# One level of Strassen's scheme in the first matmul of three feed-forwards

## The chip, the core and the metric

The kernel runs on one core of a Trainium2 chip. The metric is the device time of the program in microseconds (us), the median of a few runs. One execution was recorded by the hardware profiler; all rows below are from it. PE is TensorE's matmuls, PEld its weight loads, DVE is VectorE, ACT ScalarE, SP the engine whose queue issues the DMAs.

## The reference

Two transformer-like blocks on 512 tokens of 1024 features, float32: the first has two layers (pooling, latent attention and a linear recurrence, gated and summed), the second one layer (a state-space branch and a dilated attention). Each of these three layers ends in a feed-forward of 4096 hidden features, and the change is in these:

```
# first block, twice
h = rms_norm(x, g_ffn[l])
x = x + jnp.square(jax.nn.relu(h @ w_ff1[l])) @ w_ff2[l]
# second block, once
h = layer_norm(alpha * h + mix, ln1_g, ln1_b)
f = jnp.square(jax.nn.relu(h @ w_up)) @ w_down
h = layer_norm(alpha * h + f, ln2_g, ln2_b)
```

## The kernel before

Activations lie with features on the 128 partitions and the 512 tokens along the columns: 1024 features are eight tiles of 128 x 512. Each float32 number is held as a high and a low part that the matmul takes in one pass, so that a product of two tiles is three matmuls (`mm3`: high x high, high x low, low x high). `split` makes the parts: ScalarE copies the high part, VectorE subtracts it from the number for the low part. `X` holds the eight pairs of input tiles (`xh`, `xl`).

Weights come as panels of 128 x 1024 in the order of use. `load` takes a raw slot (class W, 4 slots), issues one DMA on SP's queue, and splits the panel into two tiles of class H (8 slots). A panel of the first matmul (`ff1`, `up`) holds the eight stationary blocks for 128 hidden features; `mmk` runs 8 x 3 = 24 matmuls over it, each of 128 rows, 128 stationary columns and 512 tokens, into one PSUM bank. Working tiles are of class T (57 slots of 128 x 528), PSUM has eight banks (class P).

`ffn` (L986) goes over four chunks of 1024 hidden features. In a chunk it makes eight hidden tiles (24 matmuls, ReLU on ScalarE, square on VectorE, split), then multiplies them by eight panels of the second matmul (`ff2`, `dn`) and adds the results to eight sums `acc`. The last chunk's second matmul goes over the token halves one after the other (`parts`), in 256 columns, and its results go to `last` and `done`, which close the layer. In the second block the first four panels of `up` are also run by token halves (`mmh`, `head=4`), so that TensorE has work on the first half while the layer norm of the second is made (`layer_norm`, `done1` in `out2`).

Ahead of the feed-forward, `mix1` runs the output projection: for each of eight tiles 24 matmuls, then VectorE adds the residual, ScalarE and VectorE split the sum with the gain `g_ffn` into `xh`, `xl`, and the sum stays in a T tile (`xn`) until the end of the feed-forward. The scale 1/rms of a token is put in at the end, since ReLU squared lets it pass.

The program is recorded first and then ordered by a list scheduler (`order`) that knows rough costs and the number of slots of each class; loads and splits of weights get a lead of 250 instructions. Each engine then runs its list in that order. The scheduler may move a plain copy from ScalarE to VectorE and back (`other`). All instructions are emitted in one place, so they carry the line L505; the groups of the profile are told apart by tiles.

Of the kernel before, what the change touches and what calls it, by code (L numbers as in the profile page):

```python
# [7 lines left out]
F32 = mybir.dt.float32  # L8
# [34 lines left out]
# ---------------------------------------------------------------- small vectors, one column per 128 features  # L43
# [65 lines left out]
def cells(v):  # L109
    """The parts of its tile that a view covers: halves of the partitions by blocks of 128 columns."""  # L110
# [19 lines left out]
# from an instruction's end to the start of one that waits for it on another engine, ns  # L130
# [19 lines left out]
class Prefix:  # L150
    """Point updates, and the least prefix sum over the first n positions."""
# [19 lines left out]
    def low(self, n):  # L171
        """min over k <= n of the sum of the first k positions."""
# [14 lines left out]
class Recorder:  # L187
# [8 lines left out]
    # -- tiles  # L196
    def open(self, sizes):
        """sizes: class -> (count, columns, space). A slot takes one tile after the other, of either type."""
        self.sizes, self.pools, self.protos = sizes, {}, {}
        for c, (n, cols, space) in sizes.items():  # L200
            p = self.tc.tile_pool(name=f"sl{c}", bufs=1, space=space, reuse_waits="tile")
            self.pools[c] = p, p.__enter__()
            for dt in (F32,) if c in "PSW" else (F32, F32R):
                self.protos[c, dt] = self.place(c, 0, dt)
# [40 lines left out]
    def record(self, eng, meth, args, kw):  # L245
# [43 lines left out]
        o.pri = i - (self.LEAD if i > 200 and isinstance(outs[0], View) and outs[0].tile.cls in ("W", "H") else 0)  # L289
# [1354 lines left out]
```

## Time and profile before

| what | value |
|---|---|
| median of three runs | 2553.19 us (2552.67 to 2555.08) |
| span of the profiled execution | 2552.5 us |
| TensorE busy | 2528.0 us, 12166 matmuls |
| VectorE busy | 1600.6 us |
| ScalarE busy | 1067.0 us |
| weights and scratch read from HBM | 241.39 MB |

Busy time is the union of an engine's instructions. A matmul's recorded duration includes its way through the array and overlaps the next one, so the pace of matmuls is read from the starts of two rows, not from their mean duration. The three feed-forwards stand at 365.61 to 724.32, 1078.18 to 1448.20 and 2167.58 to 2544.60 us of the span.

### The profile page before, as it was taken

To read this page: it belongs to the slowest core of one execution; us is meant where nothing else is said; L and a number is where in the kernel's file an instruction comes from. 1 tells how busy PE (TensorE), PEld (TensorE's weight loads), DVE (VectorE), ACT (ScalarE), POOL (GpSimd) and SP (SyncE) were. 2 spreads that over 40 slices of the span, in tenths; PEclk is the share of its full clock that TensorE was granted. 3 is DMA by queue.
4 is the path that set the end of the run, shared out by engine and by line. 5 is a ranking of instruction groups with operands and counts; after the bars stand their busy time and mean duration, and the time that the engine had idled before them with its cause. 6 is when DMAs were issued, how large, how long until landed. Compare 5 with 4: busy or idle time off the path is not lost.

```text
span 2552.5 us, 31172 instructions
## 1 busy us (share of the span) xinstructions
PE 2528.0 (99%) x12166; PEld 2063.3 (81%) x12166; DVE 1600.6 (63%) x2708; ACT 1067.0 (42%) x1796; POOL 0.2 (0%) x4
## 2 busy tenths in 40 slices
PE   8999999999999999999999999999999999999997
PEld 6888888888888888888888977777778789888887
DVE  7878554433578685544345747688999787633455
ACT  5545343322335453333233334356755743522332
POOL 0000000000000000000000000000000000000000
PEclk9999999999999999999999999999999999999998
DMA  4123332222331223323233221334422442222231
GB/s 156 64 81 96 119 100 91 96 94 95 116 110 56 81 91 122 93 91 99 92 102 121 77 75 50 100 110 151 133 91 99 149 165 83 69 97 92 102 104 34
DMA packets 83971, 251.93 MB, mean 99 GB/s; under 512 B 9520, under 2 KB 12720, under 8 KB 83824
## 3 DMA queue, kind: packets, MB, share of 16 engines
q1 hardware_dynamic: 83824, 249.95, 30.2%
q8 instruction: 95, 1.56, 0.2%
q14 instruction: 52, 0.43, 0.1%
HBM read 241.39 MB, written 8.52 MB: 98 GB/s over the span
## 4 chain that ended last, share of the span: by engine, by line
PE 97%; DVE 1%; ACT 1%; issue 0%; DMA 0%; SPq 0%; ACTq 0%; DVEq 0%
PE P L505 97%; DVE T L505 1%; ACT T L505 1%; DVE H L505 0%; DVE S L505 0%; DMA T<-in_x_dram 0%; ACT H L505 0%; ACT L505 0%; DVE xl L505 0%; SPq L505 0%; ACT xh L505 0%; ACTq L1640 0%; DVE xh L505 0%; DVEq L505 0%; ACTq L505 0%
## 5 line engine op out<-in xcount | busy, mean ns | idle before, releaser
L505 PE MATMUL P<-xh,H 128*128 128x512 f32 (+1 forms) x3912 | 1257.9, 396 | 8.8 <-DVE xh L505 6.1
L505 DVE TENSOR_TENSOR H<-W,H 128x1024 fp32r<-128x1024 f32 (+1 forms) x395 | 477.0, 1213 | 649.2 <-PE P L505 436.3
L505 PE MATMUL P<-T,H 128*128 128x512 f32 (+1 forms) x3924 | 880.2, 378 | 0.0
L505 PEld LDWEIGHTS P<-xh,H 128*128 128x128 f32 x3912 | 725.8, 189 | 181.0 <-issue 12.3
L505 ACT ACTIVATE H<-W 128x1024 fp32r<-128x1024 f32 (+1 forms) x389 | 407.5, 1052 | 1002.0 <-PE P L505 931.7
L505 PEld LDWEIGHTS P<-T,H 128*128 128x128 f32 x3924 | 695.2, 188 | 145.4 <-issue 1.5
L505 PE MATMUL P<-xl,H 128*128 128x512 f32 (+1 forms) x1968 | 772.2, 395 | 1.1 <-DVE xl L505 0.9
L505 PEld LDWEIGHTS P<-xl,H 128*128 128x128 f32 x1968 | 371.6, 189 | 87.0 <-issue 5.5
L505 DVE TENSOR_TENSOR T<-T,T 128x512 f32<-128x512 f32 (+5 forms) x600 | 363.4, 622 | 27.3 <-ACT T L505 13.1
L505 PE MATMUL P<-T,T 128*128 128x256 f32 (+7 forms) x1536 | 279.0, 311 | 0.0
L505 ACT ACTIVATE T<-T 128x512 fp32r<-128x512 f32 (+4 forms) x329 | 191.4, 591 | 164.5 <-DVE T L505 158.1
L505 PEld LDWEIGHTS P<-T,T 128*128 128x128 f32 (+2 forms) x1536 | 210.7, 184 | 37.2 <-issue 17.1
L505 ACT ACTIVATE T<-P 128x512 f32<-128x512 f32 (+6 forms) x281 | 148.9, 549 | 153.1 <-PE P L505 152.6
L505 DVE TENSOR_TENSOR T<-T,P 128x512 f32<-128x512 f32 (+2 forms) x190 | 109.3, 578 | 51.7 <-PE P L505 36.4
L505 DVE TENSOR_TENSOR T<-P,T 128x512 f32<-128x512 f32 (+5 forms) x224 | 131.4, 612 | 12.4 <-PE P L505 7.4
L505 ACT ACTIVATE T<-T,T 128x128 f32<-128x128 f32 (+1 forms) x320 | 121.2, 455 | 11.1 <-DMA T<-fscr 9.1
L505 DVE TENSOR_TENSOR T<-T 128x512 f32<-128x512 f32 (+3 forms) x109 | 75.3, 692 | 50.3 <-ACT T L505 50.2
L505 DVE SCALAR_TENSOR_TENSOR T<-T,P 128x512 f32<-128x512 f32 (+1 forms) x120 | 67.4, 575 | 29.0 <-PE P L505 23.2
L505 PE MATMUL P<-c,T 128*128 128x128 f32 (+1 forms) x436 | 74.0, 271 | 0.2 <-ACT T L505 0.2
L505 DVE SCALAR_TENSOR_TENSOR T<-P,half,T 128x510 f32<-128x510 f32 (+1 forms) x96 | 70.3, 743 | 0.6 <-ACT T L505 0.3
L505 PEld LDWEIGHTS P<-c,T 128*128 128x128 f32 (+1 forms) x436 | 54.5, 140 | 14.7 <-DVE T L505 0.9
L505 DVE SCALAR_TENSOR_TENSOR T<-T,T 128x512 f32<-128x512 f32 (+2 forms) x69 | 46.8, 685 | 12.7 <-ACT T L505 11.9
(74 smaller groups left out, 731.5 us busy)
## 6 DMA issues: line engine op xcount, KB each, us to landing
W<-in_w_dram SPq DMA_DIRECT2D x382, 512.0 KB, 3.4
T<-fscr SPq DMA_DIRECT2D x64, 256.0 KB, 4.8
T<-in_w_dram SPq DMA_DIRECT2D x24, 256.0 KB, 4.1
T<-in_x_dram SPq DMA_DIRECT2D x16, 256.0 KB, 4.7
W<-in_w_dram SPq DMA_DIRECT2D x10, 384.0 KB, 3.1
T<-in_c_dram SPq DMA_DIRECT2D x8, 256.0 KB, 4.5
xscr<-T SPq DMA_DIRECT2D x8, 256.0 KB, 2.2
T<-xscr SPq DMA_DIRECT2D x8, 256.0 KB, 3.9
```

The lines of the kernel that those rows point to most:

```text
L505: self.out(o, getattr(getattr(self.nc, o.eng), o.meth)(*[res(a) for a in o.args], **{k: res(v) for k, v in o.kw.items()}))
```

## The change

The first matmul of a feed-forward takes two panels together, 256 hidden features, and splits it as a 2 x 2 product of blocks: the features in pairs of tiles, the hidden features in two halves of 128, and the tokens in two halves of 256. Of the eight block products of this shape it makes seven, in Winograd's form, from sums of weight blocks and sums of token halves. Each product is a sum over four pairs of input tiles, three matmuls each: 12 matmuls of 256 columns. In one layer of the first block 16 pairs of panels are made so; in the second block 14, since its first four panels are still run as before.

- `wforms` loads two panels, makes four sums of 512 columns on VectorE, and splits seven forms of 512 columns.
- `xforms` makes the sums of token halves for two input tiles, and splits them; two of the forms overwrite the second half of an `X` tile. It runs in the output projection of the first block and in the layer norm of the second.
- `up` runs the seven products into three PSUM tiles. One of them (`a`) collects four products and is copied out by ScalarE after each of three and at the end; VectorE adds the other two.
- ReLU squared is now one VectorE instruction, max(u, 0) x u, or min for the tile that comes out negated.
- `ffn` records four pairs first, and then one pair after every second panel of the second matmul; the hidden tiles of the next chunk are made while those of this chunk are used.
- Classes W and H become one class W of 16 slots.
- The residual sum goes to a scratch in HBM (`rscr`) and is read back at the end of the feed-forward; in the second block the scaled residual is made in the layer norm.

```
-            self.open({"T": (57, T + 16, SB), "W": (4, 1024, SB), "H": (8, 1024, SB), "S": (48, 8, SB), "P": (8, T, PSUM)})
+            self.open({"T": (57, T + 16, SB), "W": (16, 1024, SB), "S": (48, 8, SB), "P": (8, T, PSUM)})
...
+    def wforms(self, name, p):
...
+        for i, t in enumerate((r1, r2)):
+            self.S.dma_start(t, bass.AP(tensor=self.wp.tensor, offset=off + (2 * p + i) * P * w, ap=[[w, P], [1, w]]))
...
+        a11, a22, a12, a21 = r1[:, L], r1[:, R], r2[:, L], r2[:, R]
+        f11, f12 = both(a11), both(a12)
+        s1 = add(a22, a21)
+        s2 = add(s1, a11)
+        g2, g1 = both(s2), both(s1)
+        s3 = add(a11, a21)
+        g3, f22 = both(s3), both(a22)
+        return f11, f12, both(add(s2, a12)), f22, g1, g2, g3
...
+    def xforms(self, j, v1, v2, raw=True):
...
+        t, u = self.F(), self.F()
+        V.tensor_tensor(t[:, L], v1[:, L], v1[:, R], op=ALU.subtract)
+        V.scalar_tensor_tensor(u[:, L], t[:, L], -1.0, v2[:, R], op0=ALU.mult, op1=ALU.subtract)
+        V.tensor_tensor(u[:, R], v2[:, R], v1[:, R], op=ALU.subtract)
+        V.scalar_tensor_tensor(t[:, R], u[:, L], -1.0, v2[:, L], op0=ALU.mult, op1=ALU.subtract)
+        if raw:
+            self.split(t[:, L], h1[:, R], l1[:, R])
+        g = self.splitR(u)
...
+    def product(self, ps, w, q, start, stop):
+
+        for j in range(4):
+            b = slice(j * P, (j + 1) * P)
+            self.mm3(ps, w[q][0][:, b], w[q][1][:, b], *self.G[j][q], start and j == 0, stop and j == 3, skip_group_check=True)
+
+    def up(self, name, p):
...
+        self.product(a, w, 0, True, False)
+        A.activation(f[:, L], a, AF.Copy)
+        self.product(b, w, 1, True, True)
+        V.tensor_tensor(f[:, L], f[:, L], b, op=ALU.add)
+        self.product(a, w, 5, False, False)
+        A.activation(f[:, R], a, AF.Copy)
+        self.product(c, w, 4, True, False)
+        self.product(a, w, 6, False, False)
+        A.activation(g[:, R], a, AF.Copy)
+        V.tensor_tensor(g[:, R], g[:, R], c, op=ALU.add)
+        self.product(a, w, 3, False, True)
+        A.activation(g[:, L], a, AF.Copy)
+        self.product(c, w, 2, False, True)
+        V.tensor_tensor(f[:, R], f[:, R], c, op=ALU.add)
+        return f, g
...
+        for i in range(4):
+            up(i)
+        for ch in range(3):
             for c in range(8):
-                if ch == 3:
-                    break
                 ps = self.PS()
-                self.mmk(ps, self.load(n2, ch * 8 + c), hid)
+                self.mmk(ps, self.load(n2, ch * 8 + c), hids[ch])
...
+                if c % 2 == 0:
+                    up(4 * ch + 4 + c // 2)
```

What the scheduler makes of it, at two places. TensorE near the start of the first feed-forward, before: the end of the first panel and the start of the second; `ones` and `c` stand for the sums over the partitions and the broadcast of the scale.

```order
L505 MATMUL P_767_3350<-xh_78,H_756_3274 128x512
L505 MATMUL P_767_3350<-xh_80,H_748_3204 128x512
L505 MATMUL P_767_3350<-xl_81,H_748_3204 128x512
L505 MATMUL P_767_3350<-xh_80,H_756_3274 128x512
L505 MATMUL P_775_3396<-c_62,S_773_3390 128x128 x4
L505 MATMUL P_777_3403<-xh_66,H_753_3241 128x512
L505 MATMUL P_777_3403<-xl_67,H_753_3241 128x512
L505 MATMUL P_777_3403<-xh_66,H_761_3311 128x512
```

After, in the same feed-forward where pairs and down-panels alternate: the end of one product into the PSUM tile P_946 and the start of the next into it.

```order
L505 MATMUL P_946_4293<-T_815_3528,W_926_4177 128x256
L505 MATMUL P_946_4293<-T_817_3540,W_926_4177 128x256
L505 MATMUL P_946_4293<-T_815_3528,W_926_4177 128x256
L505 MATMUL P_959_4382<-T_850_3737,W_939_4256 128x512
L505 MATMUL P_959_4382<-T_852_3749,W_939_4256 128x512
L505 MATMUL P_959_4382<-T_850_3737,W_945_4291 128x512
L505 MATMUL P_959_4382<-T_843_3702,W_939_4256 128x512
L505 MATMUL P_959_4382<-T_845_3714,W_939_4256 128x512
L505 MATMUL P_959_4382<-T_843_3702,W_945_4291 128x512
L505 MATMUL P_946_4293<-T_757_3211,W_928_4200 128x256
L505 MATMUL P_946_4293<-T_759_3219,W_928_4200 128x256
```

Before, each bank is filled once and left; after, six matmuls of a down-panel (P_959) stand between two products into the same tile.

VectorE at the end of the output projection of the first layer, before: P_762 is the eighth projection's result, xl_81 the low part that the first panel needs last.

```order
L505 TENSOR_TENSOR H_761_3311<-W_744_3175,H_753_3241 128x1024
L505 TENSOR_TENSOR T_671_2744<-P_757_3276,T_671_2744 128x512
L505 SCALAR_TENSOR_TENSOR xl_79<-T_671_2744,vec,xh_78 128x512
L505 TENSOR_TENSOR T_735_3111<-T_735_3111,T_765_3332 128x512
L505 TENSOR_TENSOR H_766_3348<-W_749_3212,H_758_3278 128x1024
L505 TENSOR_TENSOR T_681_2792<-P_762_3313,T_681_2792 128x512
L505 SCALAR_TENSOR_TENSOR xl_81<-T_681_2792,vec,xh_80 128x512
```

After, from the addition of the eighth projection's result (P_792) on:

```order
L505 TENSOR_TENSOR T_696_2875<-P_792_3406,T_696_2875 128x512
L505 TENSOR_TENSOR W_802_3457<-T_768_3268,W_802_3457 128x512
L505 TENSOR_TENSOR T_808_3487<-T_801_3453,W_775_3309 128x512
L505 SCALAR_TENSOR_TENSOR T_811_3498<-T_799_3436,T_807_3480 128x256
L505 TENSOR_TENSOR W_809_3491<-T_780_3341,W_809_3491 128x512
L505 TENSOR_TENSOR xl_81<-T_807_3480,xh_80 128x512
L505 TENSOR_TENSOR T_811_3498<-T_807_3480,T_796_3424 128x256
L505 TENSOR_TENSOR T_739_3120<-T_739_3120,T_812_3507 128x512
L505 SCALAR_TENSOR_TENSOR T_799_3436<-T_811_3498,T_807_3480 128x256
L505 TENSOR_TENSOR T_817_3540<-T_811_3498,T_815_3528 128x512
L505 TENSOR_TENSOR W_816_3536<-W_737_3109,W_816_3536 128x512
L505 TENSOR_TENSOR xl_79<-T_799_3436,xh_78 128x256
```

Before, the low part follows the addition at once; after, weight sums, low parts of weights (W) and combinations of token halves (T_811, T_799) stand between, and the second half of xl_79 is written anew at the end.

## Rows read from the trace of the kernel before

**Rows 1.** The page's parts 1 and 2: span, busy time by engine, clock in 40 slices.

```profile
span 2552.5 us, 31172 instructions
PE 2528.0 (99%) x12166; PEld 2063.3 (81%) x12166; DVE 1600.6 (63%) x2708; ACT 1067.0 (42%) x1796; POOL 0.2 (0%) x4
...
PEclk9999999999999999999999999999999999999998
```

**Rows 2.** The page's part 4, the chain that ended last.

```profile
PE 97%; DVE 1%; ACT 1%; issue 0%; DMA 0%; SPq 0%; ACTq 0%; DVEq 0%
```

**Rows 3.** TensorE's waits: for whom, us in total, times, the longest.

```profile
PE P L505 <- DVE xh L505: 6.1, 1, 6.1
```

**Rows 4.** Windows: length, busy PE, PEld, DVE, ACT, POOL, clock, DMA share, GB/s.

```profile
320.90:365.61 44.71, 44.71 (x195) 36.23 (x193) 24.90 (x32) 17.87 (x24) 0.00 (x0) 1.00 0.32 105
365.61:724.32 358.71, 358.71 (x1554) 290.17 (x1552) 162.10 (x193) 113.64 (x144) 0.00 (x0) 1.00 0.31 100
1078.18:1448.20 370.02, 370.02 (x1832) 309.76 (x1831) 175.04 (x268) 115.43 (x160) 0.00 (x0) 1.00 0.30 96
2167.58:2544.60 377.02, 368.64 (x1880) 311.36 (x1878) 183.56 (x311) 123.52 (x188) 0.00 (x0) 0.99 0.24 81
```

**Rows 5.** Windows of matmuls of 512 columns alone: a down stretch, an up stretch.

```profile
412.18:456.66 44.48, 44.48 (x194) 36.03 (x192) 15.37 (x17) 9.60 (x10) 0.00 (x0) 1.00 0.30 95
456.66:501.44 44.78, 44.78 (x193) 36.09 (x192) 20.13 (x24) 16.30 (x22) 0.00 (x0) 1.00 0.29 94
```

**Rows 6.** Matmuls of 256 columns: timeline of PE (start, length), then windows.

```profile
2487.08 11.59 PE L505 MATMUL P<-T,H 128*128 128x256 f32 x96
2498.51 11.45 PE L505 MATMUL P<-T,T 128*128 128x256 f32 x96
...
2487.08:2498.51 11.43, 11.43 (x97) 11.42 (x96) 5.73 (x9) 1.23 (x2) 0.00 (x0) 1.00 0.01 2
2498.51:2509.80 11.29, 11.29 (x99) 11.29 (x97) 3.39 (x8) 0.00 (x0) 0.00 (x0) 1.00 0.01 1
```

**Rows 7.** Groups by shape, whole span: count, busy us, mean ns, idle before.

```profile
L505 DVE TENSOR_TENSOR H<-W,H 128x1024 fp32r<-128x1024 f32 x382 | 465.9, 1224 | 644.3 <-PE P L505 431.5 <-issue 210.3 <-ACT H L505 1.3
L505 ACT ACTIVATE H<-W 128x1024 fp32r<-128x1024 f32 x376 | 397.5, 1060 | 978.9 <-PE P L505 916.8 <-issue 55.7 <-DMA W<-in_w_dram 3.9
L505 DVE TENSOR_TENSOR T<-T,T 128x512 f32<-128x512 f32 x290 | 193.0, 685 | 8.0 <-ACT T L505 5.6 <-PE P L505 0.3
L505 ACT ACTIVATE T<-T 128x512 fp32r<-128x512 f32 x178 | 111.0, 630 | 63.6 <-DVE T L505 60.6
L505 DVE TENSOR_TENSOR T<-T,P 128x256 f32<-128x256 f32 x80 | 33.0, 418 | 36.0 <-PE P L505 35.3
L505 ACT ACTIVATE T<-P 128x256 fp32r<-128x256 f32 x23 | 8.8, 387 | 4.7 <-PE P L505 4.7
```

**Rows 8.** Timeline of DVE: queued instructions of one shape, start and length.

```profile
181.99 1.89 DVE L505 TENSOR_TENSOR T<-T,T 128x512 fp32r<-128x512 f32 x3
...
2535.68 1.42 DVE L505 SCALAR_TENSOR_TENSOR T<-P,T 128x256 f32<-128x256 f32 x4 [0.79 <-PE P L505]
```

**Rows 9.** Timeline at the start of the first feed-forward, PE, DVE and ACT.

```profile
365.61 0.39 PE L505 MATMUL P<-xh,H 128*128 128x512 f32 x1
...
366.72 0.68 DVE L505 TENSOR_TENSOR T<-P,T 128x512 f32<-128x512 f32 x1
368.20 0.75 DVE L505 SCALAR_TENSOR_TENSOR xl<-T,vec,xh 128x512 fp32r<-128x512 f32 x1 [0.79 <-ACT xh L505]
...
367.44 0.72 ACT L505 ACTIVATE xh<-T,vec 128x512 fp32r<-128x512 f32 x1 [0.52 <-DVE T L505]
```

**Rows 10.** The layer norm before the third feed-forward: PE with its waits; a window.

```profile
2181.86 0.71 PE L505 MATMUL P<-c,S 128*128 128x128 f32 x4 [0.67 <-DVE S L505]
2184.10 0.88 PE L505 MATMUL P<-xh,H 128*128 128x256 f32 x4 [1.53 <-ACT xh L505]
...
2185.10:2188.60 3.50, 3.50 (x19) 3.50 (x20) 3.13 (x9) 3.40 (x8) 0.00 (x0) 0.59 0.02 5
```

More of the change, by code (lines that the diff above doesn't have):

```diff
@@ L202, in open @@
             self.pools[c] = p, p.__enter__()
-            for dt in (F32,) if c in "PSW" else (F32, F32R):
+            for dt in (F32,) if c in "PS" else (F32, F32R):
                 self.protos[c, dt] = self.place(c, 0, dt)
@@ L288, in record @@
         o.alt = self.other(o)
-        o.pri = i - (self.LEAD if i > 200 and isinstance(outs[0], View) and outs[0].tile.cls in ("W", "H") else 0)
+        o.pri = i - (self.LEAD if i > 200 and isinstance(outs[0], View) and outs[0].tile.cls == "W" else 0)
         self.ops.append(o)
@@ L548, in load, with both, add @@
         return lambda a, b: (hi[:, a:b], lo[:, a:b])
+    def wforms(self, name, p):
+        V, off, w = self.V, WOFF[name][0], 1024
+        r1, r2 = self.new("W", w), self.new("W", w)
+        for i, t in enumerate((r1, r2)):
+            self.S.dma_start(t, bass.AP(tensor=self.wp.tensor, offset=off + (2 * p + i) * P * w, ap=[[w, P], [1, w]]))
+        L, R = slice(0, T), slice(T, w)
+        def both(x):
+            hl = self.new("W", w, F32R)
+            self.split(x, hl[:, L], hl[:, R])
+            return hl[:, L], hl[:, R]
+        def add(a, b):
+            o = self.F()
+            V.tensor_tensor(o, a, b, op=ALU.add)
+            return o
+        a11, a22, a12, a21 = r1[:, L], r1[:, R], r2[:, L], r2[:, R]
[6 more added lines that the diff above has]
+        return f11, f12, both(add(s2, a12)), f22, g1, g2, g3
@@ L593, in stack, with mm3 @@
         return t
[L595 removed]
+    def mm3(self, out, lh, ll, rh, rl, start, stop, **kw):
         mm = self.E.matmul
[L597 to L599 removed]
+        mm(out, lh, rh, start=start, stop=False, **kw)
+        mm(out, lh, rl, start=False, stop=False, **kw)
+        mm(out, ll, rh, start=False, stop=stop, **kw)
     def mmk(self, out, w, xs, off=0, toks=None):
@@ L1429, in proj, with mid @@
             add(c, t, tk)
+        y2 = [self.F() for _ in range(8)]
+        self.G, t1 = [None] * 4, []
+        def mid():
+            for j, t in enumerate(t1):
+                self.split(t, *(x[:, HALVES[1]] for x in X[2 * j]))
         def done1(tk):
@@ L1436, in fin @@
                 V.tensor_tensor(X[k][1][:, tk], v, h.bitcast(F32), op=ALU.subtract)
+                A.activation(y2[k][:, tk], v, AF.Copy, scale=ALPHA)
+                if tk.start and k % 2:
+                    t1.append(self.xforms(k // 2, y[k - 1], y[k], False))
             return self.layer_norm([v[:, tk] for v in y], sums[tk.start], "ln1_g", fin, tk.start > 0)
         self.parts("out2", 0, HALVES, proj, done1)
-        y2 = self.residual()
         def last(c, acc, tk):
@@ L1457, in done @@
             return self.layer_norm([v[:, tk] for v in y2], sums[tk.start], "ln2_g", fin2, tk.start > 0)
-        self.ffn("up", "dn", HALVES, last, done, head=4, acc=y2)
+        self.ffn("up", "dn", HALVES, last, done, y2, 4, mid)
     def residual(self):
@@ L1508, in _tiles, with _quads @@
     return [np.concatenate([_fm(w, slice(c * P, (c + 1) * P), K, P) for c in range(a, a + per)], axis=1) for a in range(0, n, per)]
+def _quads(w):
+    out = []
+    for c in range(0, w.shape[1], 256):
+        a, b = (_fm(w, slice(c + i, c + i + P), 8, P).reshape(P, 4, 2, P) for i in (0, P))
+        for i in range(2):
+            out.append(np.concatenate([x.reshape(P, T) for x in (a[:, :, i], b[:, :, 1 - i])], axis=1))
+    return out
 def _bd(w, j):
```

79 lines of the change are left out of this document (53 added, 26 removed).

## The prediction

> **What bounds the kernel now.** The page comes first. TensorE is busy 99% of the span, VectorE 63%, ScalarE 42%, and TensorE's clock is granted in full nearly throughout [rows 1]. The chain that ended last lies on TensorE for 97% [rows 2]. Its longest wait for another engine is 6.1 us, at the program's start [rows 3]. Then the stretches: in the three feed-forwards TensorE is busy for all of 358.71 and 370.02 us and for 368.64 of 377.02, while VectorE works for under half of each [rows 4]. So a matmul column taken from TensorE there shortens the program, as long as the other engines keep handing over in time; and VectorE has some 190 us to spare in each.
>
> The profiled execution spans 2552.5 us [rows 1]; the median of the runs is 2553.19, 0.7 us outside the span. The sum below is taken off 2553.2.
>
> **TensorE's work.** Two hidden blocks (256 hidden features) take two panels of 24 matmuls of 512 columns before, and seven products of 4 x 3 = 12 matmuls of 256 columns after: 48 large against 84 small. What matters is the pace, start to start, in stretches with one shape only. 512 columns: the eight up-panels (24 matmuls each) from 456.66 to 501.44 take 44.78 us for 192, 233.2 ns each; the down-panels from 412.18 to 456.66 take 231.7 [rows 5]. 256 columns, one weight load per matmul as in the change: 96 from 2487.08 to 2498.51, 119.1 ns; 96 from 2498.51 to 2509.80, 117.6 [rows 6]. So half the columns cost half the time, within 2%. I take 118.3, the middle of the two, since the products draw their moving side from both kinds of tile.
>
> Per pair of panels: 48 x 233.2 = 11.19 us goes, 84 x 118.3 = 9.94 comes: 1.26 us won. There are 16 pairs in each of the first two feed-forwards and 14 in the third (its first four panels stay): 46 x 1.257 = **57.8 us**. At 119.1 ns it is 54.7, at 117.6 it is 60.5. The break-even pace is 11.19 / 84 = 133 ns.
>
> The Trainium skill, "TensorE: Matmul & The Clock Gate", section "Back-to-back issue gap", speaks against the change: for a stream of weight loads and matmuls it gives about 81 ns at 128 columns and 131 at 512, so a large fixed part. An estimate from that page, by a straight line, is 98 ns at 256, so 84 x 98 = 8.2 us against 48 x 131 = 6.3, and 46 x 1.9 = 87 us lost. The trace disagrees, with 233 and 118 ns.
>
> **VectorE and ScalarE.** Prices from the rows: VectorE 685 ns for 512 columns, 418 for 256, 1224 for 1024; ScalarE 630, 387 (out of PSUM) and 1060 [rows 7]. Queued VectorE instructions overlap: three of 512 columns end after 1.89 us, so 0.60 each after the first; four of 256 after 1.42, so 0.33 [rows 8]. A pair of panels now needs on VectorE 7 low parts, 4 sums, 2 squares and 2 low parts of the hidden tiles, 15 x 0.60, and 3 sums out of PSUM, 3 x 0.33: 10.0 us, nearly 11 with the ScalarE copies that the planner shifts over (87 out of PSUM and 25 of 512 columns, over 46 pairs). ScalarE: 9 x 0.63 + 4 x 0.39 = 7.2 us, less those. In the middle of a feed-forward two down-panels (48 x 231.7 = 11.1 us) stand between pairs: TensorE 21.1 us, VectorE 11 + 2 x (1.14 + 0.60) = 14.5. Covered, with 6 us over; extra work here costs nothing. The eight writes and eight reads of 256 KB for the residual, on SP's queue, hide too: nothing on TensorE waits for them, and the DMA share in a feed-forward is 0.31 [rows 4].
>
> **The openings of the first two feed-forwards.** Four pairs run without down-panels between: TensorE 4 x 9.94 = 39.8 us, VectorE 40 to 44. Ahead of them, in the output projection, VectorE is busy 24.90 of 44.71 us [rows 4], so 19.8 free. The new combinations of the moving side take 9.3 of that (per two tiles two instructions of 512 columns and seven of 256, two of these some 0.07 longer, 3.65 us by [rows 8], against two of 0.67 before; four times). So some 10 us of weight sums can be done ahead, which is more than the 4 missing, but VectorE runs at 90% over 84 us. The critical place is the last pair of moving tiles. Before, the last projection panel ends its issue at 365.61; VectorE adds at 366.72, ScalarE makes the high part at 367.44, VectorE the low part by 368.95, and TensorE needs it at 370.5, after 21 matmuls [rows 9]: 1.5 us spare. After, the order shows four instructions between the addition and that low part, 2.8 us with the addition: if the addition starts 1.1 us after the panel's end as before, the low part is there at 1.1 + 2.8 + 0.7 = 4.6 us; TensorE has 39 small matmuls queued before it, 4.6 us. The second half of the tile before needs six more instructions and its own, to 7.5 us; TensorE has 59 small matmuls and four short ones queued, 7.4 us. So nothing is spare where 1.5 us was, and each semaphore's delay, or a late VectorE, shows. I take 1.5 us for each of the two openings; bounds 0 and 5.
>
> **The opening of the third.** Before, TensorE stands 0.67 and 1.53 us around the layer norm of the second token half, and the granted clock is 0.59 over the next 3.5 us [rows 10]: 1.3 us more, since 19 matmuls run there where 30 would fit. After, 24 matmuls (the first two products of the first pair, which read the first token half alone) stand before the broadcast, 2.8 us, and cover the first gap. But then VectorE makes per two tiles 3.85 us of work (two gains of 0.40, two low parts of 0.33, six combinations and low parts of 2.4) where it made 1.46: 15.4 us for four pairs, begun 2.2 us after the broadcast (2181.86 to 2184.10). In the order 136 small matmuls, 16.0 us, stand between the broadcast and the first product that needs the last of it: 1.6 us short. The second gap and its slow clock stay, the first gap goes, and I add 1.5 for semaphores along eight tiles: 1.6 + 1.5 - 0.67, some 2.5 us lost; bounds -2 (both gaps and most of the slow clock gone) and 6.
>
> **The hand-offs inside a pair** are a wait that the trace of before doesn't have. One PSUM tile collects four products and is copied out after each of the first three; the next product into it waits for the copy. The order puts 12 small matmuls (1.42 us) in each of the first two gaps, and six large ones of a down-panel in the third, 1.39 us. The need is the drain of the last matmul (0.16: it ends 0.28 after its start, the next starts 0.118 after) and the 387 ns copy [rows 7], some 0.6 with the semaphores. It is covered unless the copy stands behind another ScalarE instruction: behind a split of 1060 ns the need is 1.6 and 0.2 us is lost. ScalarE is busy for less than half the time, and the planner puts the copies in their place. 46 x 3 = 138 hand-offs: I take 2 us; bounds 0 and 10. Who is queued behind such a copy is the other splits of weights; those have the 6 us.
>
> The merged weight pool gives 16 slots to loads and splits that had 4 and 8. It moves the order of the other stages a little (three quarters or more of TensorE's order there stays). TensorE is full there, so nothing is to be won; I take 0 and 3 us either way. Nothing else on the path changes: the last chunk's second matmul and the closing norm stand as they were.
>
> **Sum:** -57.8 + 2 x 1.5 + 2.5 + 2.0 = -50.3, and 2553.2 - 50.3 = **2503**.
>
> **The rivals.**
> - The gain comes whole: the small matmuls run at 117.6 everywhere and the openings cost nothing, 2553.2 - 60.5 = 2493. For it: TensorE has no idle time in 729 us of the first two feed-forwards, so the planner's order leaves room. Against it: VectorE's 90% at the openings.
> - VectorE bounds more than the openings. Hidden tiles of two chunks, sums and combinations hold 16 + 16 + 8 + 12 + 1 = 53 of 57 tiles at the end of a chunk, so the weight sums of the last pair (nine such places) may not be made ahead, and up to 11 x 0.6 = 6.6 us of them stand open: at half that, 30 us, 2533. Against it: weight slots, not tiles, hold the finished forms, and VectorE has 6 us over per pair.
> - The slower one: hand-offs. Where a hand-off loses more than 57.8 / 138 = 0.42 us on the mean, the gain is gone. With a 1060 ns split always in front of the copy and only four large matmuls as cover (0.93 us) it is 0.7 us: 138 x 0.7 = 97 us, 2592. For it: the copies share ScalarE's queue with every weight split. Against it: the covers of 1.4 us.
> - A fixed part per matmul: the pace at 256 columns doesn't halve when weights come fresh from VectorE all the time. Weight loads then leave no gap (11.29 of 11.29 us busy at 256 columns, 36.09 of 44.78 at 512 [rows 5, 6]), so any slowing shows at once. At 145 ns: 46 x 84 x 26.7 ns = 103 us, 2606. Against it: both pure stretches, in one of which VectorE is busy half the time. The page's rule cited above is of this kind, and would make it slower still, 2640.
>
> **Chances.** Forecast (2496 to 2513) 0.68; whole gain 0.12; tiles and VectorE, or late openings, 2513 to 2545: 0.13; hand-offs 0.04, fixed part 0.03. The two last end on the slow side or near zero. About 0.2% is what a measurement of this kernel tells from no change (5 us). So faster 0.93, same 0.02, slower 0.05. The range that leaves out 2 in 10: 2491 to 2522.
>
> **What would show it.** In the trace after: three feed-forwards of some 341 (358.7 - 16 x 1.257 + 1.5 + 0.7), 352 and 362 us; 3864 more matmuls of 256 columns and 2208 fewer of 512, the small ones 117 to 120 ns apart; VectorE busy near 70% there; TensorE's waits for ScalarE's tiles, absent now, under 0.1 us each; idle time of TensorE mostly in the first 15 us of each opening. I am wrong if the small matmuls stand over 125 ns apart inside a product, or if waits of TensorE repeat in each pair.

## The result and the profile after

The changed kernel takes **2487.47 us** (median of four runs, 2487.01 to 2488.91) where the kernel before, beside it, takes 2554.04. The ratio is 0.9742 (95% interval 0.9728 to 0.9756): 66.6 us gained where 50.3 were forecast. The sign and the mechanism were right, the size was not, and the time lies below the forecast's range. The profiled execution spans 2487.1 us.

The page's part 1 and the chain that ended last (part 4) after the change, to be held against [rows 1, 2]:

```profile
span 2487.1 us, 35399 instructions
PE 2462.5 (99%) x13822; PEld 2098.7 (84%) x13822; DVE 1911.1 (77%) x3451; ACT 1157.8 (47%) x2067; POOL 0.2 (0%) x4
...
PE 98%; DVE 1%; ACT 1%; issue 0%; DMA 0%; SPq 0%; ACTq 0%; DVEq 0%
```

TensorE has 1656 more matmuls (3864 small ones, of 256 columns, more and 2208 large ones, of 512, fewer) and is still the bound; VectorE went from 63% to 77%. The three feed-forwards as windows, with the columns of [rows 4]:

```profile
364.73:700.65 335.92, 335.92 (x2130) 302.69 (x2129) 256.08 (x415) 138.38 (x220) 0.00 (x0) 1.00 0.37 114
1054.63:1400.16 345.53, 345.53 (x2391) 320.44 (x2390) 266.27 (x490) 140.99 (x231) 0.00 (x0) 1.00 0.34 110
2120.72:2479.10 358.38, 349.19 (x2383) 322.24 (x2382) 272.18 (x525) 144.51 (x261) 0.00 (x0) 0.98 0.28 89
```

Against 358.71, 370.02 and 377.02 they are 22.8, 24.5 and 18.6 us shorter, 65.9 together; all the rest of the program moved by 0.5. The first two have no idle time of TensorE. TensorE's waits, to be held against [rows 3] (the first four of seven lines and the last):

```profile
PE P L505 <- DVE xh L505: 6.3, 1, 6.3
PE P L505 <- DVE T L505: 3.1, 3, 1.9
PE P L505 <- DVE S L505: 2.4, 1, 2.4
PE P L505 <- ACT T L505: 2.0, 1, 2.0
...
PE P L505 <- DVE W L505: 0.3, 1, 0.3
```

The only wait for a combination of the moving side on ScalarE is a single one of 2.0 us, in the third opening, and no copy out of PSUM is waited for at any of the 138 hand-offs. In the timeline of TensorE the third opening has these idle stretches (in brackets):

```profile
2138.93 0.74 PE L505 MATMUL P<-xh,W 128*128 128x256 f32 x4 [1.53 <-ACT xh L505]
2139.94 0.38 PE L505 MATMUL P<-xl,W 128*128 128x256 f32 x1 [0.27 <-DVE xl L505]
...
2159.20 1.91 PE L505 MATMUL P<-T,W 128*128 128x256 f32 x13 [2.00 <-ACT T L505]
```

The wait of 0.67 us before the broadcast [rows 10] is gone, that of 1.53 behind it stands, and the granted clock still falls after it (0.55 from 2140.00 to 2143.80, 0.59 before). The 2.00 is the late last combination.

Summed from start to start over the trace, the small matmuls of the products stand 116.4 ns apart (116.42, 116.86 and 115.95 in the three feed-forwards, without the few over 150 ns), not 118.3. By the tile that the moving side lies in: those from T tiles stand at some 118.3, as was taken for all, and those from xh/xl at some 115.1. That is the question of the experiments: what set this pace, and did anything else carry part of the gain?

### The profile page after: what moved, and what is told of

It reads as the page before. It is cut to its first block, busy times and chain, and to the rows that moved or that the text cites. A ratio compares the mean times of both kernels' runs of the same rounds, so it can differ in the third digit from the quotient of the medians.

```text
span 2487.1 us, 35399 instructions
## 1 busy us (share of the span) xinstructions
PE 2462.5 (99%) x13822; PEld 2098.7 (84%) x13822; DVE 1911.1 (77%) x3451; ACT 1157.8 (47%) x2067; POOL 0.2 (0%) x4
## 4 chain that ended last, share of the span: by engine, by line
PE 98%; DVE 1%; ACT 1%; issue 0%; DMA 0%; SPq 0%; ACTq 0%; DVEq 0%
PE P L505 98%; DVE T L505 1%; ACT T L505 1%; DMA T<-in_x_dram 0%; DVE W L505 0%; ACT W L505 0%; DVE S L505 0%; DVE xl L505 0%; SPq L505 0%; ACTq L1765 0%; ACT xh L505 0%; DVE xh L505 0%; DVEq L505 0%; ACTq L505 0%
## 5 line engine op out<-in xcount | busy, mean ns | idle before, releaser
L505 PE MATMUL P<-T,W 128*128 128x512 f32 (+1 forms) x5580 | 1100.2, 349 | 2.0 <-ACT T L505 2.0
L505 PE MATMUL P<-xh,W 128*128 128x512 f32 (+1 forms) x3912 | 1064.8, 351 | 8.1 <-DVE xh L505 6.3
L505 PEld LDWEIGHTS P<-T,W 128*128 128x128 f32 x5580 | 894.6, 188 | 142.5 <-ACT T L505 2.9
L505 PEld LDWEIGHTS P<-xh,W 128*128 128x128 f32 x3912 | 681.6, 189 | 114.1 <-issue 12.2
L505 PE MATMUL P<-xl,W 128*128 128x512 f32 (+1 forms) x1968 | 685.6, 351 | 1.2 <-DVE xl L505 1.2
L505 DVE TENSOR_TENSOR W<-W,W 128x1024 fp32r<-128x1024 f32 (+2 forms) x441 | 460.1, 1046 | 250.3 <-PE P L505 126.6
L505 ACT ACTIVATE W<-W 128x1024 fp32r<-128x1024 f32 (+2 forms) x424 | 386.8, 915 | 548.8 <-PE P L505 492.0
L505 PEld LDWEIGHTS P<-xl,W 128*128 128x128 f32 x1968 | 371.3, 189 | 55.6 <-issue 5.5
L505 DVE TENSOR_TENSOR T<-T,T 128x512 f32<-128x512 f32 (+6 forms) x636 | 378.9, 614 | 23.8 <-ACT T L505 14.1
L505 ACT ACTIVATE T<-T 128x512 fp32r<-128x512 f32 (+5 forms) x365 | 207.5, 578 | 250.2 <-DVE T L505 240.3
```

What stands on the lines that cost most here:

```text
L505: self.out(o, getattr(getattr(self.nc, o.eng), o.meth)(*[res(a) for a in o.args], **{k: res(v) for k, v in o.kw.items()}))
```

## Experiments

Each time is a median, with the ratio's interval to the kernel before of the same chip (2552.8 to 2553.1 us).

### Is the gain the products' own?

The products replaced by ordinary panels. What belongs to the products alone goes with them (the combinations of token halves, ReLU squared as one instruction); the rest of the change is kept. The host lays the first weights out for pairs of panels, and the plain panels read them as they lie, so they compute other sums of the same size.

```
-    for u, op in zip(self.up(n1, i), (ALU.max, ALU.min)):
...
+    for j in (2 * i, 2 * i + 1):
...
+        self.mmk(ps, self.load(n1, j), self.X)
...
```

> The changed kernel with ordinary panels of 24 matmuls of 512 columns in place of the seven products: the interleaving of first and second matmul, the one weight pool, the way of the residual through memory and its later scaling stay. Theory (all of the gain is the products' own): the time of before, 2554.0 less the 0.9 us that after was ahead at the start of the first feed-forward, 2553 within 2. Rival (the interleaving or the pool carries the part of the gain that the prediction missed, some 8 us): 2546.

2550.43 us, ratio 0.9991 (0.9982 to 1.0000): 2.3 us of the gain, between 0 and 4.6, are not the products'. Its windows:

```profile
364.22:723.04 358.82, 358.82 (x1554) 290.25 (x1553) 166.71 (x203) 102.80 (x136) 0.00 (x0) 1.00 0.33 107
1076.82:1444.57 367.75, 367.75 (x1815) 307.51 (x1814) 175.48 (x273) 107.14 (x153) 0.00 (x0) 1.00 0.33 103
2165.27:2540.66 375.39, 367.26 (x1879) 309.73 (x1878) 182.36 (x311) 111.02 (x174) 0.00 (x0) 0.99 0.24 80
```

The first is as before. The second is 2.3 shorter because the first matmuls of the next stage no longer stand among its last (block 2 is 1.3 longer for it); the third gains 1.6 at its opening. So the 24.5 us of the second window above hold some 2 that are only a border moved.

One weight pool alone, in the kernel before:

```
-  "W": (4, 1024, SB), "H": (8, 1024, SB)
+  "W": (12, 1024, SB)
...
```

> The kernel before with one weight pool of 12 slots in place of the pools of 4 and 8, nothing else. Theory (the pool only shifts the start of the program, where after and the kernel without the products are 0.2 to 1.4 us ahead at the first feed-forward): 2552.8 less 0 to 1.5. Rival (the pool carries the whole 2.3 us that the kernel with the change's order but ordinary panels gained): 2550.5 within 0.5.

2555.30 us, 1.0009 (1.0000 to 1.0018): the pool by itself gains nothing; it may cost up to 4.6 us. Neither theory had that sign. The prediction's 0 with 3 either way holds it.

### Do VectorE and the hand-offs limit it?

The interleaving undone:

```
-    if c % 2 == 0:
-        up(4 * ch + 4 + c // 2)
+    if c == 7:
+        for i in range(4):
+            up(4 * ch + 4 + i)
```

> The changed kernel without the interleaving: the four pairs of a chunk stand together behind the eight down-panels of the chunk before, so each of nine more places has four pairs without cover. Theory (four pairs together take TensorE 4 x 84 x 116.7 ns = 39.2 us and VectorE 40 to 44, and the 16 weight slots let part of the forms be made ahead under the down-panels): 0.5 to 2 us lost at each of nine places, 2492 to 2505. Rival (VectorE is never late by itself, the planner's order makes up for it): 2487.5 within 2. Rival (VectorE's weight sums stand open as in the prediction's second rival, 3 to 6.6 us at nine places): 2515 to 2547.

2488.42 us, 0.9748 (0.9734 to 0.9761), so the first rival: nothing lost. The first feed-forward has no idle time here either:

```profile
365.44:701.47 336.03, 336.03 (x2130) 302.41 (x2129) 256.12 (x415) 137.87 (x221) 0.00 (x0) 1.00 0.37 116
```

VectorE works ahead in part: from 415 to 450 us, under down-panels alone, it makes 12 weight sums and the low parts of 10 forms; 4 sums and 21 low parts follow from 450 to 485, while products run. That the prediction's second rival (VectorE and tiles) fell is shown; that the interleaving is worth nothing is shown for this order only.

Each copy of a hand-off done twice:

```
     A.activation(f[:, L], a, AF.Copy)
+    A.activation(f[:, L], a, AF.Copy)
```

> The changed kernel with each of the three copies out of the shared PSUM tile done twice in a row, so that each of the 138 hand-offs needs about 1.0 us where it needs 0.6, and ScalarE has 138 x 0.39 = 54 us more to do. Theory (the hand-offs are covered by 12 small or six large matmuls, 1.4 us, and cost nothing in the trace of after): 2487.5 within 1, and no wait of TensorE for these copies. Rival of the prediction (copies stand behind other ScalarE work, each hand-off near its limit): 0.2 to 0.4 us at each of 138, 2515 to 2542.

2494.90 us, 0.9771 (0.9758 to 0.9785): 7 us more than the changed kernel, between the two. The windows are 337.81, 346.50 and 360.48; beside the changed kernel the intervals over 150 ns add 0.6, 0.8 and 1.2 us, about 19 ns for each of 138 hand-offs; the rest is other paces and 1.6 us in block 2, whose order moved. Doubled hand-offs start to show; single ones do not.

VectorE loaded with 173 us of sums that nobody uses:

```
+    for _ in range(8 if p >= 4 else 0):
+        add(a11, a12)
```

> The changed kernel with eight more sums of 512 columns (of no use) among the weight sums of each of the 36 pairs that stand between down-panels: VectorE gets 8 x 0.60 = 4.8 us more per pair, 173 us in all, less than the 6 us per pair that the prediction called spare (21.1 us of TensorE against 14.5 of VectorE). Theory (VectorE is covered there): 2487.5 within 2. Rival (the 6 us are not there, since forms must come early or ScalarE's and VectorE's work is tied together): each us that VectorE lacks shows 36 times, 2500 or more.

2492.10 us, 0.9763 (0.9750 to 0.9776), 4.6 us more, where the theory allowed 2 and the rival asked for 12 or more. VectorE's busy time in the first feed-forward rises from 256.08 to 300.48 of 336.95 us (the planner gave some copies to ScalarE):

```profile
363.84:700.79 336.95, 336.95 (x2130) 303.10 (x2129) 300.48 (x483) 150.44 (x249) 0.00 (x0) 1.00 0.38 115
```

So 44 us more of VectorE's time, 3.7 for each of twelve pairs, lengthened TensorE's work by 1.0 us there. That much of the 6 us per pair that the prediction called spare was spare; the rest of it was not tried.

### What sets the pace of a small matmul?

Eight half-size products in the kernel before, all from xh/xl:

```
-  self.ffn(..., last, done)
+  self.ffn(..., last, done, head=32)
```

> The kernel before, with every up-panel of the three feed-forwards taken by token halves (48 matmuls of 256 columns where 24 of 512 stood), so eight half-size products where the change has seven, all from xh/xl, and nothing else of the change. Theory (my term priced the small matmuls too high: from xh/xl they run at 114.8 ns): per pair 96 x 114.8 = 11.02 us against 11.19, over 46 pairs 8 us less than before, 2546. Rival (the 118.3 ns of the prediction holds and the gain beyond it comes from elsewhere): 96 x 118.3 = 11.36, 7.5 us more, 2561.5.

2549.34 us, 0.9985 (0.9976 to 0.9994): 3.4 us less, between the two theories, or 115.8 ns. The trace shows why: whole chunks (384 matmuls each) stand at one of two paces, 45.23 / 384 = 117.8 and 43.53 / 384 = 113.4 ns, with the same shape, tiles and neighbours:

```profile
457.42:502.65 45.23, 45.23 (x386) 45.22 (x384) 20.11 (x25) 16.30 (x22) 0.00 (x0) 1.00 0.32 94
636.77:680.30 43.53, 43.53 (x385) 43.52 (x384) 20.10 (x23) 16.33 (x22) 0.00 (x0) 1.00 0.33 97
```

The products of the changed kernel that draw from T tiles made to draw from xh/xl:

```
+    q2 = {3: 0, 5: 1, 6: 2}.get(q, q) if self.pairno >= 4 else q
-    ... *self.G[j][q] ...
+    ... *self.G[j][q2] ...
```

> The changed kernel, but in the pairs 4 to 15 of each feed-forward the products 3, 5 and 6 draw their moving side from the constant xh/xl tiles (of products 0, 1 and 2) and not from the T tiles with the combinations; the combinations are still made, so only the operand's place changes, and the output means nothing. Theory (the pace of a 256-column matmul depends on where its moving tile lies: 114.8 ns from xh/xl, 118.7 from T tiles, by the trace of after): 36 pairs x 36 matmuls x 3.9 ns = 5.1 us less than after's 2487.5, so 2482.4, and 114 to 116 ns inside these products. Rival (the products 3, 5 and 6 are slower for their place in the order, their PSUM tile or their neighbours): 2487.5 within 1, and 118 to 119 ns still.

2487.02 us, 0.9744 (0.9730 to 0.9757): no gain. Matched by their place in the order, the changed matmuls fell from some 118.2 to 116.2 ns, much as the theory wanted, but those of products 0, 1, 2 and 4 rose from 115.2 to 115.9 and took about half of it back. The kind of tile is not the cause by itself.

The changed kernel once more:

> The changed kernel once more, unaltered, for a second trace of the same program. In the first traces whole products, and in the half-panel run whole chunks, stand at one of two paces from the same tiles: 113.3 or 117.8 ns from start to start. Theory A (the pace belongs to the program: slots, order): the same products stand at the same pace as in the first trace, product by product, mean 116.4 again. Theory B (it belongs to the execution): other products stand at 113.3 than before, and the mean moves by up to 1 ns in a feed-forward, some 1.3 us of 1344 matmuls. Time 2487 within 1.5 by both.

2488.86 us. The means are 116.38, 116.86 and 115.87. In the first two feed-forwards this is theory A: all but 28 of some 2870 intervals of small matmuls lie within 2.5 ns of what they were. Two stretches of 24 matmuls (products 0 and 1 of two pairs), in the first trace and then in the second:

```profile
432.02:434.85 2.83, 2.83 (x26) 2.83 (x25) 2.52 (x3) 1.97 (x3) 0.00 (x0) 1.00 0.16 20
...
495.01:497.74 2.73, 2.73 (x25) 2.73 (x24) 2.64 (x3) 1.73 (x4) 0.00 (x0) 1.00 0.01 3
```

```profile
430.78:433.61 2.83, 2.83 (x26) 2.83 (x24) 2.52 (x3) 1.97 (x3) 0.00 (x0) 1.00 0.13 23
493.77:496.51 2.74, 2.74 (x26) 2.74 (x24) 2.65 (x3) 1.73 (x4) 0.00 (x0) 1.00 0.01 3
```

Some 117.8 ns and some 113.9 both times. The third feed-forward is not so: 133 of some 1520 intervals differ, most of them behind its opening. In the first execution the granted clock fell there, at 2140 us; in the second it stayed full there, and fell some 20 us later, behind the next wait (0.54 from 2158.00 to 2161.50). Sixteen of these matmuls, in the first trace and then in the second:

```profile
2154.00:2155.89 1.89, 1.89 (x19) 1.89 (x18) 1.61 (x4) 1.89 (x5) 0.00 (x0) 1.00 0.56 147
2151.28:2153.10 1.82, 1.82 (x19) 1.82 (x17) 1.82 (x5) 1.82 (x5) 0.00 (x0) 1.00 0.53 164
```

So the program sets the pace where no wait disturbs it, but the same matmuls at the same addresses can stand at either of the two paces (117.8 and 113.3 ns here), and which one they take can hang on what came before. What of the program? The next four kernels keep the order, instruction by instruction, and move addresses alone. What counts below is the shift: how many bytes the weights lie behind the moving tile in a partition, modulo 256. In the changed kernel, and in the one before, the 57 T tiles of 2112 bytes lie between xh/xl and the weight slots, and 57 x 2112 is 64 more than a multiple of 256: against xh/xl the weights stand at a shift of 64, against T tiles, one after the other, at 0, 64, 128 and 192.

```
e9, halves:    xh/xl tiles of T + 16 columns, 2112 bytes apart
e10, halves:   32 bytes before xh0: all tiles move alike
e11, changed:  the same
e12, changed:  32 bytes behind xl7: T tiles and weights move against xh/xl
```

> The half-panel kernel with the same order, instruction by instruction, but the sixteen xh/xl tiles lie 2112 bytes apart in a partition, as the T tiles do, and not 2048. Theory (which of the paces a stream of 256-column matmuls takes is set by the addresses of the moving tiles from one matmul to the next): the steady 113.3 and 117.8 ns go, each interval takes its own value between 112 and 123 as from T tiles, about 118 in the mean, and the 4414 matmuls that stood at 115.6 take 10.6 us more, 2560. Rival (the addresses don't matter; something in the stream's past sets the level): the same level in the same chunk as before, 2549 within 1.5.

> The half-panel kernel with the same order, but all tiles from xh0 on (xh/xl, the T tiles, the weights) lie 32 bytes higher. Theory (addresses relative to each other set the levels): each chunk at the level it had, 2549 within 1.5. Rival (where a tile lies against a line of 64 bytes counts: all these tiles began 32 bytes into one, now at its start): other levels, and if a line's start is better 113.3 for most: 4414 x 2.3 ns = 10 us less, 2539.

> The changed kernel with the same order, but all tiles from xh0 on lie 32 bytes higher. Theory (relative addresses alone): the products at the paces they had, mean 116.4, 2487.5 within 1.5. Rival (alignment to 64 bytes): paces change; at 113.3 throughout, 3864 x 3.1 ns = 12 us less, 2475.5.

> The changed kernel with the same order; the xh/xl tiles stay and the T tiles and the weights lie 32 bytes higher. Theory (the relation of weights and moving tiles sets the level): products 0, 1, 2 and 4, from xh/xl, change their levels while 3, 5 and 6, whose tiles moved with the weights, keep their 118.7 mean; the mean over all by up to 2 ns either way, 2480 to 2495. Rival (no relation): the paces of the trace of after, 2487.5 within 1.5.

e9: 2556.38 us, 1.0013 (1.0004 to 1.0022), 7.0 more than the halves. Every chunk now takes 118.9 ns; the second:

```profile
456.67:502.31 45.64, 45.64 (x386) 45.64 (x384) 20.12 (x25) 16.31 (x22) 0.00 (x0) 1.00 0.32 93
```

e12: 2497.65 us, 0.9784 (0.9770 to 0.9797), 10 more than the changed kernel for 32 bytes. Products 0, 1, 2 and 4 go to 117.6, 118.1 and 118.5 ns in the three feed-forwards (from 114.7, 115.8 and 114.9), 3, 5 and 6 stay near 118; the stretch that took 2.73 us above takes 2.82:

```profile
495.77:498.59 2.82, 2.82 (x25) 2.82 (x24) 2.73 (x3) 1.81 (x4) 0.00 (x0) 1.00 0.01 3
```

e11: 2490.42 us, 0.9754 (0.9741 to 0.9768); its paces are those of the changed kernel (116.40, 116.86, 115.95); its trace is 1.4 us longer, nearly all of that in the third feed-forward, and 0.7 of it waits. e10: 2545.95 us, 0.9972 (0.9962 to 0.9983): all relations kept, yet the second chunk stands at 113.4 where it had 117.8, and the first of the third feed-forward the other way round:

```profile
456.76:500.29 43.53, 43.53 (x385) 43.52 (x384) 20.12 (x25) 16.34 (x22) 0.00 (x0) 1.00 0.34 97
```

So the relation of the weights' address to the moving tile's sets which paces are possible; which of two stands at a shift of 64 is not settled by it.

Then the pace by itself, on an otherwise idle core, in one execution:

```
for r in range(8):
    for j in range(4):      # d: shift of the weights, pitch: distance of moving tiles
        matmul(o, W[hi, j, d], M[2 * j, pitch]); matmul(o, W[hi, j, d], M[2 * j + 1, pitch])
        matmul(o, W[lo, j, d], M[2 * j, pitch])
```

> No part of the reference is computed: TensorE alone runs streams of 96 matmuls (one product eight times: four pairs of tiles, three matmuls each, every one with its own weight load), first of 256 and then of 512 columns, the moving tiles 2048 bytes apart. From stream to stream the weights move by 32 bytes against the moving tiles, over 512 bytes up and back down; then 256 and 512 columns once more with the tiles 2112 bytes apart. Nothing else runs. Theory (the address of a matmul's weights against its moving tile sets its pace): at 256 columns some shifts stand at 113.3 ns, some at 117.8 or more, the same on the way up and down, and the tiles 2112 bytes apart at some 118.9; at 512 columns 225 to 241. Rival (other engines' accesses to the same memory make the difference): one pace, 113.3 at all shifts, since nothing else runs here. Rival (the past of a stream sets it): shifts that differ on the way up and down.

Seven of its 102 streams (96 matmuls each): 256 columns at a shift of 64, of 224 (up), of 224 (down) and of 0; then 512 columns at 64, 0 and 256:

```profile
36.76:48.07 11.31, 11.31 (x99) 11.31 (x97) 0.00 (x0) 0.00 (x0) 1.00 0.01 1
93.68:104.99 11.31, 11.31 (x98) 11.31 (x97) 0.00 (x0) 0.00 (x0) 1.00 0.01 1
309.97:321.18 11.21, 11.21 (x99) 11.21 (x97) 0.00 (x0) 0.00 (x0) 1.00 0.01 1
389.32:400.83 11.51, 11.51 (x99) 11.51 (x97) 0.00 (x0) 0.00 (x0) 1.00 0.00 0
1090.54:1112.94 22.40, 22.40 (x97) 18.06 (x96) 0.00 (x0) 0.00 (x0) 1.00 0.00 0
1135.34:1157.12 21.78, 21.78 (x97) 18.02 (x96) 0.00 (x0) 0.00 (x0) 1.00 0.00 1
578.98:600.75 21.77, 21.77 (x97) 18.02 (x96) 0.00 (x0) 0.00 (x0) 1.00 0.00 1
```

117.8, 117.8, 116.8 and 119.9 ns; 233.3, 226.9 and 226.8. Both rivals fall as main causes: the paces differ with nothing else running, and they repeat every 256 bytes, up and down, but for a shift of 128 and, at 256 columns, of 224, where the past moves them by 1 ns. The steady 113.3 did not appear, so these streams do not account for the 115.1 of the products from xh/xl. For T tiles in the changed kernel, which go through four shifts, the streams give (120.0 + 117.8 + 119.3 + 117.8) / 4 = 118.7 ns, and 118.7 and 118.2 were measured in the first two feed-forwards; for 512 columns from xh/xl, at 64, they give 233.3, and [rows 5] has 233.2.

### Tiles placed by that table

```
-  "T": (57, T + 16, SB)        # 2112 bytes apart
+  "T": (57, T, SB)             # 2048; the tiles of 528 columns go to weight slots
+  fix([16], "pad")             # 64 bytes behind xl7: in the first only
```

> The changed kernel with T tiles of 512 columns, 2048 bytes apart (the few tiles of 528 columns stand in weight slots), and 64 bytes between xh/xl and T, so that T tiles stand at 0 and xh/xl at 64, modulo 256 bytes, against the weights. The order of the work shifts a little outside the feed-forwards. Theory (the paces of the streams by themselves, 226.7 ns at 0 for 512 columns and 120.0 for 256): the 1920 matmuls of 512 columns in the feed-forwards 231.3 to 226.7, 8.8 us less; products 3, 5 and 6 from 118.7 to 120, 2 us more; the out projections and other matmuls of 512 columns from T tiles some 5 us less: 2473 to 2483, faster than both kernels. Rival (the pace in the whole kernel hangs on the other engines' accesses): 231 as before, 2487.5 within 2.

> The same without the 64 bytes: xh/xl stand at 0 against the weights too. Theory: products 0, 1, 2 and 4 slow down from 115.2 to 120, 2208 x 4.8 ns = 10.6 us more than the kernel with the 64 bytes. Rival (their pace hangs on something else): the same time as with them, within 2.

> The kernel before with T tiles of 512 columns, so that xh/xl and T tiles stand at 0 against the weights. Theory: the 2208 up matmuls from 233.3 to 226.7, 14.6 us less; the 1920 down matmuls of 512 columns 8.8 less; other stages some 5 less: 2519 to 2528, so that most of 30 us, near half of what the change brought, is to be had in the old kernel from addresses alone. Rival (addresses matter only for small matmuls): 2552 within 2.

The kernel before: 2521.53 us, 0.9877 (0.9863 to 0.9890), as the theory said: 31 us with the same 12166 matmuls. A down and an up stretch, 226.7 ns each, to be held against [rows 5]:

```profile
414.14:457.66 43.52, 43.52 (x194) 36.04 (x192) 15.36 (x17) 9.62 (x10) 0.00 (x0) 1.00 0.32 97
457.66:501.18 43.52, 43.52 (x194) 36.04 (x192) 20.11 (x24) 16.31 (x22) 0.00 (x0) 1.00 0.32 97
```

The changed kernel with all tiles at 0: 2486.70 us, 0.9742 (0.9728 to 0.9755), the time that it had. Its large matmuls run at 227.9 ns and other stages gain (the first feed-forward starts at 359.91, not 364.73), but its small ones take 119.8. With the 64 bytes: 2491.59 us, 0.9760 (0.9747 to 0.9773), a miss of 8 us and more. TensorE's order is the same in both. The paces came near what was expected, 227.7 ns for its downs and 117.3 for its small matmuls. But the gain of the other stages, which comes from xh/xl at 0, did not come: its first feed-forward starts at 363.96. So the kernel without the 64 bytes, expected 10.6 us slower, was 4.9 faster. And both lost in the third opening, because the moved tiles changed the planner's order; in the kernel with the 64 bytes TensorE waits there for ScalarE's weight forms:

```profile
PE P L505 <- ACT W L505: 6.0, 3, 4.3
```

So large matmuls want 0 and small ones do not. The last two keep all tiles at 0 and move only the products' weights inside slots of 1088 columns (the planner's lead for loads also became 260, which moves the order a little):

```
-    hl = self.new("W", w, F32R)
-    self.split(x, hl[:, L], hl[:, R])
+    hl = self.new("W", None, F32R)
+    hi, lo = hl[:, 16:528], hl[:, 528:1040]        # e18: 56:568, 568:1080
+    self.split(x, hi, lo)
```

> The kernel with T and xh/xl tiles at 0 against the panels of ordinary matmuls, but the weights of the seven products stand 64 bytes further in their slots (slots of 1088 columns), and the planner's lead for loads is 260 where it was 250. Theory (512 columns run best at 0, 256 columns at 64): large matmuls 226.7 ns as in the kernel without the shift, small ones from 119.8 to between 116.3 (steady pace 113.3 for part of the xh/xl streams, as in the changed kernel) and 117.8 (as the streams by themselves): 7.7 to 13.5 us less than its 2486.7, so 2473 to 2479, faster than both kernels. Rival (the relation holds for whole tiles, not for where the weights stand in a slot): 2486.7 within 2.

> The same with the products' weights 224 bytes further in their slots. Theory by the streams by themselves (116.7 to 117.8 ns at 224): 3864 x 2.0 to 3.1 ns = 7.7 to 12 us less than 2486.7, so 2475 to 2479. Rival: 2486.7 within 2.

2472.53 us, 0.9684 (0.9671 to 0.9697), and **2471.66 us, 0.9682 (0.9669 to 0.9695)**: faster than both kernels, some 15 us faster than the changed one. Both are under the theory's lower end, by 0.5 and 3.3. The small matmuls of the second stand at 116.7 ns (117.3 in the third feed-forward), the large ones at 228.0. Against the kernel with all tiles at 0 it is 15.0 us faster: 3864 x (119.8 - 116.9) = 11.2 are the pace of the small matmuls, some 2 a better third opening. Its windows:

```profile
360.33:694.33 334.00, 334.00 (x2130) 303.07 (x2129) 247.74 (x394) 142.55 (x233) 0.00 (x0) 1.00 0.35 112
1044.00:1388.17 344.17, 344.17 (x2390) 320.88 (x2389) 263.26 (x481) 143.69 (x239) 0.00 (x0) 1.00 0.34 110
2100.91:2461.87 360.96, 350.12 (x2383) 324.74 (x2382) 264.31 (x504) 148.40 (x282) 0.00 (x0) 0.99 0.25 85
```

Each kernel in its better place, the products bring 2521.5 - 2471.7 = 49.9 us, not 66.6: part of the gain measured first came from large matmuls that stood in a bad place (233.3 ns for 226.7) being replaced by small ones in a fair place. By paces it is 46 x (48 x 226.7 - 84 x 116.9 ns) = 48.9. The pair is not clean: ahead of the first feed-forward, where no product runs yet, the old kernel's new order costs it some 3 us (it starts at 368.75, not 365.61), and the changed kernel starts it 4.4 us earlier than it did at first (360.33, not 364.73).

## Why the prediction was off, step by step

| Step | Taken | Measured, after against before |
|---|---|---|
| the products, 46 pairs | -57.8 | 46 x (48 x 233.3 - 84 x 116.4 ns) = -65.4 |
| openings of the first two | +3.0 | +0.2 (intervals over 150 ns: 0.79 and 0.62 against 0.61 and 0.60) |
| opening of the third | +2.5 | +1.6 |
| hand-offs | +2.0 | 0, no wait at any |
| pool, order of other stages | 0 | +2.4 for the pool alone; -2.3 (-4.6 to 0) for all but the products |

Of the 16.3 us between forecast and result 7.6 are the pace and 5.7 the allowances for openings and hand-offs; the 3.0 left are within what the last row leaves open. Neither of the two alone takes the time out of the range: 2503 - 7.6 is 2495.

- **The step that failed** is the pace: "I take 118.3, the middle of the two, since the products draw their moving side from both kinds of tile". Both stretches of [rows 6] draw from T tiles, while 2208 of the 3864 new matmuls draw from xh/xl. For T tiles the price was right (118.3), for xh/xl it was some 3 ns too high (115.1). The trace of before had small matmuls from xh/xl, and they were not priced: 70 in the first four panels of the third feed-forward, at 7.94 / 70 = 113.4 ns, and 67 behind the second, at 7.90 / 67 = 117.9:

```profile
2189.04:2196.98 7.94, 7.94 (x73) 7.94 (x71) 7.74 (x15) 7.70 (x14) 0.00 (x0) 1.00 0.13 41
1450.73:1458.63 7.90, 7.90 (x70) 7.90 (x69) 7.06 (x15) 4.27 (x8) 0.00 (x0) 1.00 0.13 36
```

  These are the two paces of the experiments, and the products took some of each. Weighted by tile, (2208 x 113.4 + 1656 x 118.3) / 3864 = 115.5 ns would have put the term at -68.7, and with 117.9 in place of 113.4 it is 118.1 ns and -58.7; -65.4 lies between. So the trace of before could give the wider range, but not the pace itself. The two ends of the range taken came from one kind of tile, so the truth lay outside both. Underneath, "half the columns cost half the time, within 2%" was a coincidence of addresses: in the streams alone, at a shift of 0, it is 120.0 against 226.7, 6% off.
- **The allowances** were 7.5 us for things without a price in the trace; 1.8 came. The third opening went as told: first gap covered, second kept, last combination late (2.0 us where 1.6 + 1.5 were worked out). At the other two the 1.5 us each did not come: TensorE has no idle time in either window. These allowances erred the same way as the pace, and that took the time below the range.
- **What held:** VectorE is covered (the run without interleaving, and for 3.7 us per pair the idle sums), the copies stay out of the way (the waits, and the doubled copies), the residual's transfers hide, and no fixed part appears. That also decides against the estimate from the Trainium skill ("TensorE: Matmul & The Clock Gate", section "Back-to-back issue gap"): its 131 ns at 512 columns stands against 226.7 to 234.3 in the streams alone.
- **The rivals:** "the gain comes whole", 2493, was nearest, and too careful for the same reason. VectorE, the hand-offs and the fixed part are out.

Not settled: why a stream at a shift of 64 settles at 113.3 in some chunks and at 117.8 in others, and what in the chip makes the 256 bytes. So why the products from xh/xl took as much of the faster pace as they did, and with it the 7.6 us, is not explained to the end; that 32 bytes more between the weights and xh/xl take it from them is shown (117.6 to 118.5 ns).

## What to carry over

Price an instruction by rows that share its operands' place as well as its shape; two rows from one pool are one row, not two ends of a range, and rows of one kind that differ (113.4 and 117.9 ns here) are a range, not a mean. Where TensorE is the bound, the distance of tiles in memory is a parameter like any other: try the pitch and offset of weights and moving tiles before and after a change of the algorithm, since a bad place can lend a change a gain that is not its own. Allowances for waits that no view shows should stay in the range, not in the sum.

## What was not expected of the hardware

- The pace of matmuls with their own weight load depends on the address of the weights against the moving tile, modulo 256 bytes, with nothing else running: 226.7 ns (shift 0) to 234.3 (shift 96) at 512 columns, 116.7 (224) to 120.0 (0) at 256, in one execution. The shift that is best for 512 columns is the worst for 256.
- Within a whole kernel, streams at a shift of 64 hold one of two steady paces, 113.3 or 117.8 ns, for chunks of 45 us. In a second execution the changed kernel held the same ones in its first two feed-forwards; behind the wait in the third's opening, where the clock fell in one execution alone, the same matmuls stood at 117.8 once and at 113.3 once.
- 32 bytes of padding cost the changed kernel 10 us (2497.65 against 2487.47); tiles placed by the table of streams gave it 15.
